# Taking the feed-forward halves' work in the order of the source, with weight splits at fixed places

## The chip, the core and the metric

The kernel runs on one core of a Trainium2 chip. Its time is device time in microseconds (us). Before the change it is 2786.39 us, the median of three runs (2783.53 to 2787.11). One further execution was recorded by the hardware profiler; it took 2785.98 us, and all rows shown here come from it.

## The reference, cut to what matters

A trunk of two layers is applied to 640 tokens (512 of a sample, 128 of a prompt) with width D = 1024. Each layer is half a feed-forward sub-layer, a mixer (attention and the like) and another feed-forward half, so there are four feed-forward halves. Each sub-layer is normalised and modulated by a shift, a scale and a gate that are computed from a condition vector.

```python
def swiglu(h, w_in, w_out):                  # w_in: 1024 x 5632, w_out: 2816 x 1024
    gate, up = jnp.split(h @ w_in, 2, axis=-1)
    return (jax.nn.silu(gate) * up) @ w_out

def adaln_sublayer(x, mod, s, g_pre, g_post, fn, weight):
    h = rmsnorm(x, g_pre) * (1 + scale) + shift
    y, aux = fn(h)
    return x + weight * gate * rmsnorm(y, g_post), aux
```

with `mod = silu(cond) @ mod_w[l] + mod_b[l]`: nine vectors of 1024 for each layer and each of two conditions.

## The kernel before

**Numbers and matmuls.** Values are float32. Every operand of a matmul is split into a high part and a remainder (`hi`, `lo`), and a product is made of three passes, hi x hi, hi x lo and lo x hi. The split of a weight block is a cast on ScalarE (ACT, line 159) and a subtraction on VectorE (DVE, line 160). The matmuls run on TensorE (PE).

**Parts and units.** The hidden width of 2816 is 22 slices of 128, called units here, and `PARTS = (2, 4, 4, 4, 4, 4)` groups them. A part computes its units' `g = silu(gate) * up` and then multiplies them with the rows of w_out that belong to them, in output products over five token tiles and two halves of the columns (matmuls of line 779, sums into `yacc` on DVE at line 804, in part 0 copies on ACT at line 802). Between the groups of output products there are places at which other things are traced: one group of matmuls, then `stream.pump()`, then `tick()`.

**Part 0** uses plain column products (matmuls of line 607) and `glu` (lines 650 to 652), whose result is split into g's two parts. `combine` then makes sums and differences of the activations' quarters (lines 662 and 665, two of the sums on GpSimd (POOL), the others on DVE) and splits them. Its eight steps are taken one at a place by `tick()`, between part 0's output products.

**Parts 1 to 5** compute gate and up of a unit together, in `strassen`, by a scheme of seven products p1, p2, p6, p5, p7, p4, p3 instead of eight, each of twelve matmuls of 128x128 by 128x320 (line 690). The order on PE for unit i of a part is p2 of i, p3 of i-1, p6, p5, p7 of i, p1 of i+1, p4 of i. p1 and p2 use one weight block of the unit (kind X), p6 one called S, p5 and p4 one called Z, p7 and p3 one called V. p1's sum is copied by ACT (line 709), p2's is added by DVE and passed through SiLU (lines 714 and 715), p6 writes onto p1's bank and ACT copies it (line 720) before p7 may write there, p7's sum is copied and added (lines 730 and 731), p4's is multiplied in (line 736), p3's is added, passed through SiLU and multiplied (lines 744 to 746). The two halves of the unit's g are then cast and subtracted (lines 352 and 353 through `out`). Behind the last unit of a part stands `fill`, the first group of output matmuls, between its p7 and p4.

**The stream of weights.** `Stream` keeps a list of all weight blocks in the order of use. Raw blocks of 512 KB are loaded over SyncE's (SP's) DMA queue into three buffers; a new load is issued when a buffer's count says that one is free. For a unit two raw blocks are loaded (gate and up), and four POOL operations (line 145) combine them into S and V's source as soon as X is split, in place in the raw buffers. `split()` makes the high and the low part of the next block in one of five buffers (`W_BUFS`). `pump()` is called between products, and also by `done()` at the end of the products that free a block. Each call splits all blocks for which there is room, but stops behind a block of a unit.

**Modulation.** The vectors for later sub-layers are computed beside the feed-forward halves, by `tick()`. `on_v` works on DVE (lines 411 and 413, 16 products of 128x512) and ends in a short PE matmul (line 425), an addition (line 428) and writes on SP's queue; one such unit is staged behind every part but the last, over the places of the output products. `on_t` works on PE (line 445, two bursts of 16 small matmuls) and is staged over the places of `strassen` in some parts. Both load their weights over SP's queue.

**What sets the order of the work.** The program is traced in the order of the source. Then a scheduler with a model of costs sets the order of each engine's instructions; within what the data allow it may put an instruction that is traced later ahead of one that is traced earlier. Each engine, and each queue that issues DMAs, then takes its instructions in that order, one after the other.

Of the kernel before, what the change touches and what calls it, by code (L numbers as in the profile page):

```python
# [60 lines left out]
class Stream:  # L61
# [9 lines left out]
    def __init__(self, nc, raw_pool, w_pool, late):  # L71
# [6 lines left out]
        self.limit = W_BUFS  # L78
        self.part_tile = None

    def add(self, key, spec):

        self.loads.append(spec)
        self.specs.append((key, spec[:2], "W", (len(self.loads) - 1,)))

    def add_unit(self, key, gate, up):
        n = len(self.loads)
        self.loads += [gate, up]
        for kind in self.UNIT:
            self.specs.append(((kind, *key), (4 if kind == "S" else 8, 128), kind, (n, n + 1)))  # L90
# [16 lines left out]
    def _room(self):  # L107
        if self.n_split == len(self.specs):
            return False
        key, _, kind, lids = self.specs[self.n_split]  # L110
        if key in self.late:
            return key in self.extra
        if len(self.held) >= self.limit:
            return False
        if kind == "S":
            return lids[0] in self.parts and self.n_pump >= self.parts[lids[0]][1] + PARTS_LAG
        return True

    def pump(self):

        self.n_pump += 1
        self._loads()
        while self._room():
            kind = self.specs[self.n_split][2]
            self.split()
            self._loads()
            self._combine()
            if kind in self.UNIT:
                break
        self._combine()  # L130

    def _combine(self):
# [58 lines left out]
def kblock(w, k0, nk, c0, n):  # L191
    return w[k0 * 128:(k0 + nk) * 128, c0:c0 + n].rearrange("(k p) n -> p k n", p=128)
# [22 lines left out]
def hybrid_flow_kernel(ctx: ExitStack, tc: tile.TileContext, I, O):  # L215
    nc = tc.nc
# [21 lines left out]
    stream = Stream(nc, wpool, wpool, late)  # L238
# [16 lines left out]
    def ffn_specs(l, j):  # L255
        wi, wo = I["ffn_w_in"][l, j], I["ffn_w_out"][l, j]
        first = not specs
        if first:

            for q in range(NK // 2):  # L260
                srcs = [(0, 128, 256 * u, kblock(wi, 2 * q, 2, u * D_FF, 256)) for u in range(2)]
                stream.add(("first", q), (2, 512, srcs))
        for p, fts in enumerate(ffn_parts()):
            for f in fts if p or not first else ():
                gate, up = (whole(kblock(wi, 0, 8, u * D_FF + f * 128, 128)) for u in range(2))
                if p:
                    stream.add_unit((l, j, f), gate, up)
                else:
                    stream.add(("in", l, j, f, 0), gate)
                    stream.add(("in", l, j, f, 1), up)  # L270
            if p < len(PARTS) - 1:
                for h in range(2):
                    for f in fts[::2]:
                        stream.add(("out", l, j, f, h), whole(kblock(wo, f, 2, h * 512, 512)))
            else:
                for f in fts:
                    stream.add(("out", l, j, f), whole(kblock(wo, f, 1, 0, 1024)))
# [69 lines left out]
    hT = [state.tile([128, NK, TOK], F32R, name=f"hT{i}") for i in range(2)]  # L347
    modrows = [[dram.tile([2, D], F32, name=f"mod{l}_{r}") for r in range(9)] for l in range(2)]
    nc.scalar.activation(out=cc, in_=craw, func=AF.Silu)

    def split(src, hi, lo):
        a = nc.scalar.copy(hi, src)  # L352
# [267 lines left out]
    def ffn(fp, l, s, pending, todo, nxt, banks0=None):  # L620
# [4 lines left out]
        j = s // 2  # L625
# [53 lines left out]
        class Unit:  # L679


            count = 0

            def __init__(self, f, g, pos, last):
                self.f, self.g, self.pos, self.last = (l, j, f), g, pos, last
# [32 lines left out]
            def p6(self):  # L718
                self.product(self.Y, self.get("S"), C[2], False)
                nc.scalar.copy(self.t[:, 1], self.Y)  # L720
                self.done("S")

            def p5(self):
# [17 lines left out]
            def p3(self):  # L741
                t = self.t
                self.product(self.Z, self.half(self.V, 1), B[1, 1], False)
                nc.vector.tensor_tensor(out=t[:, 1], in0=t[:, 1], in1=self.Z, op=ALU.add)
                nc.scalar.activation(out=t[:, 1], in_=t[:, 1], func=AF.Silu)
                nc.vector.tensor_tensor(out=t[:, 1], in0=t[:, 1], in1=t[:, 2], op=ALU.mult)
                self.out(1 if self.last else 0, 2)
                self.done("V")

            def out(self, a, b):  # L750
# [6 lines left out]
        def strassen(fts, g, fill):  # L757

            us = [Unit(f, g, i, f == fts[-1]) for i, f in enumerate(fts)]
            for i, u in enumerate(us):  # L760
                todo = [] if i else [u.p1]
                todo += [u.p2] + ([us[i - 1].p3] if i else []) + [u.p6, u.p5, u.p7]
                todo += [us[i + 1].p1, u.p4] if i + 1 < len(us) else [fill, u.p4, u.p3]
                for fn in todo:
                    fn()
                    stream.pump()
                    tick()

        stream.part_tile = part_tile
        for p, fts in enumerate(parts):  # L770
            last = p == len(parts) - 1
# [13 lines left out]
            if not last:  # L785
# [22 lines left out]
                fill = lambda: next(outs)  # L808
            else:
# [23 lines left out]
                def reload(ts, tags):  # L833
                    for t, tag in zip(ts, tags):
                        x[t] = fp.tile([128, 4, HALF], F32, tag=tag, name=tag, bufs=1)
                        x[t] = x[t].rearrange("p k n -> p (k n)")[:, 0:D]
                        src = x_saved[t]
                        if first:
                            src = I["x_sample"][0, t * 128:(t + 1) * 128, :] if t < 4 else I["x_prompt"][0]
                        nc.sync.dma_start(out=x[t], in_=src)  # L840
# [5 lines left out]
            if p == 0 and first:  # L846
                for i in range(len(fts)):
                    glu(banks0[i], g, i)
                prep += combine()
            elif p == 0:  # L850
                banks = [pair_banks() for _ in fts]
                win = []
                for i, f in enumerate(fts):
                    for u in range(2):
                        win.append(stream.get(("in", l, j, f, u)))
                        col_product(win[-1], banks[i][u], 0)
                        if (i, u) == (0, 1):
                            pending[0]()
                        elif (i, u) == (1, 0):
                            pending[1]()  # L860
                for i, f in enumerate(fts):
                    for u in range(2):
                        col_product(win[2 * i + u], banks[i][u], 1)
                        if u == 1:
                            glu(banks[i], g, i)
                        stream.done()
                prep += combine()
            else:
                if not last:
                    mod.stage("t", n_t[p], 7 * len(fts))  # L870
                strassen(fts, g, fill)
            if p == 3 and first:
                spread_bias(g[0][0])
            if not last:
                mod.stage("v", 1, 4 * len(fts) - 1)
                for _ in outs:
                    stream.pump()
                    tick()

        reload((4,), ("b40",))  # L880

        def pieces(t):
# [1284 lines left out]
```

## Time and profile before

| | |
|---|---|
| median of 3 runs | 2786.39 us (2783.53 to 2787.11) |
| profiled execution | 2785.98 us |
| its span in the trace | 2784.2 us |
| PE busy | 2563.5 us, 92% |
| DVE busy | 1845.4 us, 66% |
| ACT busy | 1178.1 us, 42% |
| POOL busy | 703.3 us, 25% |
| bytes moved by DMA | 296.95 MB, 107 GB/s on average |

The span runs from the first to the last instruction on the trace. PE is the engine of matmuls; "PEld", its loading of weights, runs beside it. "PEclk" in the profile is the clock that was granted to PE, as a share of full speed. A row of a timeline gives the start and the duration of an instruction, with its line in the kernel; "<-" names what it waited for. A row of the table of windows gives a stretch of the span, its length, the busy time and number of instructions of PE, PEld, DVE, ACT and POOL in it, the granted clock, the busy share of the DMA engines and GB/s. A row of SP's queue is the issue of a transfer (line 99 loads raw weight blocks). Idle time of an engine that nothing waits for costs nothing.

### The profile page before, as it was taken

The numbers are of one execution on the slowest core, as the hardware profiler recorded it, in microseconds if no ns is written. First come the engines' busy times: TensorE is split into PE (matmuls) and PEld (weight loads), VectorE is DVE, ScalarE is ACT, GpSimd is POOL, SyncE is SP. The second block draws the span as 40 slices with busy tenths as digits, with TensorE's granted clock in tenths as the row PEclk, the third lists the DMA queues.
The fourth block names the chain that finished last, engine by engine and source line by source line (L and its number), as shares of the span: only waits on it lengthen the run. The fifth ranks groups of instructions, "written<-read, shape, count | busy, mean of one in ns | idle before, by whom it ended". The sixth has DMA issues, their size and how long they took to land.

```text
span 2784.2 us, 40608 instructions
## 1 busy us (share of the span) xinstructions
PE 2563.5 (92%) x15930; PEld 2275.5 (82%) x15930; DVE 1845.4 (66%) x2847; ACT 1178.1 (42%) x2179; POOL 703.3 (25%) x612
## 2 busy tenths in 40 slices
PE   6898979999999989999988999999899998999998
PEld 5787868888866878888877888888899977888887
DVE  5766555675676676667568665676777768755556
ACT  4433323464455543333354333334655655333333
POOL 1222322310010032223233223123433302323222
PEclk9999999999999999999999999999999999999999
DMA  8345453421210433443343543444122223322233
GB/s 247 116 132 155 143 163 98 137 68 48 65 40 16 132 98 117 138 126 85 99 136 116 163 125 107 117 127 133 57 65 76 66 97 123 93 84 61 77 105 114
DMA packets 356697, 296.95 MB, mean 107 GB/s; under 512 B 44365, under 2 KB 289049, under 8 KB 356505
## 3 DMA queue, kind: packets, MB, share of 16 engines
q1 hardware_dynamic: 352040, 281.25, 34.0%
q10 hardware_dynamic: 2880, 9.18, 0.8%
q0 software_dynamic: 1584, 3.93, 0.5%
q8 instruction: 125, 2.05, 0.3%
q14 instruction: 68, 0.55, 0.1%
HBM read 282.24 MB, written 15.97 MB: 107 GB/s over the span
## 4 chain that ended last, share of the span: by engine, by line
PE 42%; DVE 11%; POOL 6%; ACT 4%; issue 3%; DMA 2%; DVEq 0%; ACTq 0%; POOLq 0%; SPq 0%
PE ps L690 15%; PE ps L779 13%; PE ps L607 5%; DVE wlo L160 3%; PE ps L1023 3%; POOL raw L145 3%; PE ps L597 2%; ACT whi L159 2%; POOL G L145 2%; DVE mod L413 1%; PE ps L1970 1%; DVE mod L411 1%; ACT g L352 1%; DMA mod<-in_mod_w_dram 1%; PE ps L1951 1%
## 5 line engine op out<-in xcount | busy, mean ns | idle before, releaser
L159 ACT CAST whi<-raw 128x1024 fp32r<-128x1024 f32 x400 | 418.7, 1050 | 475.9 <-PE ps L779 225.1
L779 PE MATMUL ps<-whi,g 128*128 128x512 f32 x1760 | 574.6, 403 | 40.3 <-ACT g L352 26.6
L160 DVE TENSOR_TENSOR wlo<-raw,whi 128x1024 fp32r<-128x1024 f32 x400 | 495.8, 1242 | 140.2 <-ACT whi L159 129.9
L690 PE MATMUL ps<-hT,whi 128*128 128x320 f32 x2560 | 577.1, 313 | 0.0
L145 POOL TENSOR_TENSOR raw<-raw 128x512 f32<-128x512 f32 x160 | 216.7, 1354 | 1241.2 <-DVE wlo L160 1138.3
L690 PE MATMUL ps<-b,whi 128*128 128x320 f32 x1920 | 444.4, 319 | 93.0 <-ACT xn L720 51.0
L690 PEld LDWEIGHTS ps<-hT,whi 128*128 128x128 f32 x2560 | 433.1, 191 | 12.9 <-DVE x L804 5.3
L779 PEld LDWEIGHTS ps<-whi,g 128*128 128x128 f32 x1760 | 339.7, 193 | 122.6 <-ACT g L352 29.4
L690 PEld LDWEIGHTS ps<-b,whi 128*128 128x128 f32 x1920 | 329.7, 194 | 110.4 <-ACT xn L720 61.3
L690 PE MATMUL ps<-hT,wlo 128*128 128x320 f32 x1280 | 399.6, 312 | 0.0
L779 PE MATMUL ps<-wlo,g 128*128 128x512 f32 x880 | 353.7, 402 | 0.0
L690 PE MATMUL ps<-b,wlo 128*128 128x320 f32 x960 | 303.6, 316 | 12.1 <-DVE wlo L160 12.1
L607 PE MATMUL ps<-hT,whi 128*128 128x384 f32 (+1 forms) x1216 | 277.9, 317 | 0.0
L690 PEld LDWEIGHTS ps<-hT,wlo 128*128 128x128 f32 x1280 | 244.4, 191 | 0.0
L607 PEld LDWEIGHTS ps<-hT,whi 128*128 128x128 f32 x1216 | 204.2, 189 | 21.9 <-issue 15.2
L413 DVE SCALAR_TENSOR_TENSOR mod<-mod,cc 128x512 f32<-128x512 f32 x238 | 201.0, 880 | 17.7 <-DMA mod<-in_mod_w_dram 17.7
L779 PEld LDWEIGHTS ps<-wlo,g 128*128 128x128 f32 x880 | 170.0, 193 | 37.4
L690 PEld LDWEIGHTS ps<-b,wlo 128*128 128x128 f32 x960 | 186.2, 194 | 12.4 <-DVE wlo L160 12.4
L607 PE MATMUL ps<-hT,wlo 128*128 128x384 f32 (+1 forms) x608 | 188.8, 311 | 0.0
L804 DVE TENSOR_TENSOR x<-x,ps 128x512 f32<-128x512 f32 x160 | 107.6, 685 | 92.2 <-PE ps L779 91.5
L159 ACT CAST whi<-G 128x512 fp32r<-128x512 f32 x72 | 44.7, 621 | 263.5 <-POOL G L145 152.5
L160 DVE TENSOR_TENSOR wlo<-G,whi 128x512 fp32r<-128x512 f32 x72 | 73.0, 1014 | 118.3 <-ACT whi L159 118.1
(407 smaller groups left out, 3911.0 us busy)
## 6 DMA issues: line engine op xcount, KB each, us to landing
raw<-in_ffn_w_in_dram SPq DMA_DIRECT2D x172, 512.0 KB
mod<-in_mod_w_dram SPq DMA_DIRECT2D x128, 512.0 KB
raw<-in_ffn_w_out_dram SPq DMA_DIRECT2D x88, 512.0 KB
raw<-in_na_w_qkv_dram SPq DMA_DIRECT2D x24, 512.0 KB
raw<-in_ab_w_in_dram SPq DMA_DIRECT2D x22, 512.0 KB
raw<-in_mod_w_dram SPq DMA_DIRECT2D x32, 256.0 KB
xs<-x ACTq DMA_DIRECT2D x15, 512.0 KB
b<-xs SPq DMA_DIRECT2D x15, 512.0 KB
```

Of the source, the lines that this page charges most:

```text
L145: self.nc.gpsimd.tensor_tensor(out=out, in0=in0, in1=in1, op=op)
L159: self.nc.scalar.copy(hi[:, :k * n], raw[:, :k * n])
L160: self.nc.vector.tensor_tensor(out=lo[:, :k * n], in0=raw[:, :k * n], in1=hi[:, :k * n].bitcast(F32), op=ALU.subtract)
L352: a = nc.scalar.copy(hi, src)
L411: nc.vector.tensor_scalar(out=acc[:, c], in0=raw[:, 0], scalar1=w, scalar2=None, op0=ALU.mult)
L413: nc.vector.scalar_tensor_tensor(out=acc[:, c], in0=raw[:, k % 2], scalar=w, in1=acc[:, c], op0=ALU.mult, op1=ALU.add)
L597: nc.tensor.matmul(out=banks[grp], lhsT=w[a][:, k, :], rhs=hT[b][:, k, o:o + n], start=(k == 0 and (a, b) == (0, 0)), stop=(k == NK - 1 an ...
L607: nc.tensor.matmul(out=banks[grp], lhsT=w[a][:, k, :], rhs=hT[b][:, k, o:o + n], start=(k == 0 and (a, b) == (0, 0)), stop=(k == NK - 1 an ...
L690: nc.tensor.matmul(out=out, lhsT=w[a][:, k, :], rhs=b[c][:, k, :], start=start and (k, a, c) == (0, 0, 0), stop=(k == 3 and (a, c) == PASS ...
L779: nc.tensor.matmul(out=out, lhsT=g[a][kf][:, t * 128:(t + 1) * 128], rhs=w[b], start=(kf == 0 and (a, b) == (0, 0)), stop=(kf == len(fts) ...
L804: nc.vector.tensor_tensor(out=dst, in0=dst, in1=acc[t], op=ALU.add)
L1023: nc.tensor.matmul(out=y[t][h], lhsT=hT[a][:, k, t * 128:(t + 1) * 128], rhs=ws[k // 2, h][b][:, k % 2, :], start=(k == 0 and (a, b) == (0 ...
```

## The change

A unit's four blocks are no longer split wherever `pump()` finds room. Only a part's first unit (`alone`) may be split so; any of its blocks that are still missing are split behind p1 and p2 of that unit. For the other units the source names the places: behind p2 of a unit two blocks (its own Z and V), behind p6 one (X of the next unit), behind p4 one (S of the next unit). Blocks of w_out are still split by `pump()` and `done()`. The split of the second half of g that p3 ends with is traced behind the copy in the next unit's p6 (`Unit.later`), except in a part's last unit. And `in_order` ties each instruction that is traced after part 0's activation (`mark`) to the one traced before it on the same engine, without a semaphore, up to the end of the last part's output matmuls: within that stretch of each feed-forward half the scheduler can no longer change the order on any engine.

```diff
     def _room(self):
@@
-        if len(self.held) >= self.limit:
+        if len(self.held) >= self.limit or (kind in self.UNIT and lids[0] not in self.alone):
             return False
@@
+    def unit_item(self):
+
+        kind = self.specs[self.n_split][2]
+        assert kind in self.UNIT and len(self.held) < self.limit, (self.specs[self.n_split], self.held)
+        self.split()
+        self._loads()
         self._combine()
@@
-                    stream.add_unit((l, j, f), gate, up)
+                    stream.add_unit((l, j, f), gate, up, f == fts[0])
@@
+    def in_order(last):
+
+        traced = nc.cur_bb.bb.instructions
+        n = next(i for i in reversed(range(len(traced))) if traced[i] is last) + 1
+        before = {}
+        for i in traced[:n]:
+            before[i.engine] = i
+        for i in traced[n:]:
+            if i.engine in before:
+                tc.add_manual_dep(
+                    i, before[i.engine].name,
+                    mybir.DependencyInfo(mybir.DependencyClass.NoSync, mybir.DependencyReason.DATA), reason="in_order",
+                )
+            before[i.engine] = i
@@
             def p6(self):
                 self.product(self.Y, self.get("S"), C[2], False)
                 nc.scalar.copy(self.t[:, 1], self.Y)
+                for fn in Unit.later:
+                    fn()
+                Unit.later.clear()
                 self.done("S")
@@
-                self.out(1 if self.last else 0, 2)
+                if self.last:
+                    self.out(1, 2)
+                else:
+                    Unit.later.append(lambda: self.out(0, 2))
                 self.done("V")
@@
         def strassen(fts, g, fill):
 
             us = [Unit(f, g, i, f == fts[-1]) for i, f in enumerate(fts)]
+            item = stream.unit_item
             for i, u in enumerate(us):
-                todo = [] if i else [u.p1]
-                todo += [u.p2] + ([us[i - 1].p3] if i else []) + [u.p6, u.p5, u.p7]
-                todo += [us[i + 1].p1, u.p4] if i + 1 < len(us) else [fill, u.p4, u.p3]
-                for fn in todo:
+                begin, end = i == 0, i + 1 == len(us)
+
+                todo = [(u.p1, ())] if begin else []
+                todo.append((u.p2, () if begin else (item, item)))
+                if not begin:
+                    todo.append((us[i - 1].p3, ()))
+                todo += [(u.p6, () if end else (item,)), (u.p5, ()), (u.p7, ())]
+                todo.append((fill if end else us[i + 1].p1, ()))
+                todo.append((u.p4, () if end else (item,)))
+                if end:
+                    todo.append((u.p3, ()))
+                for fn, items in todo:
                     fn()
+                    while begin and fn in (u.p1, u.p2) and stream.specs[stream.n_split][0][1:] == u.f:
+                        item()
+                    for split_next in items:
+                        split_next()
                     stream.pump()
                     tick()
@@
                 strassen(fts, g, fill)
+            if p == 0:
+                mark = nc.cur_bb.bb.instructions[-1]
@@
+        in_order(mark)
         reload((4,), ("b40",))
```

## Rows read from the trace of the kernel before

**Rows 1.** page, busy time by engine: us, share of the span, instructions

```profile
PE 2563.5 (92%) x15930; PEld 2275.5 (82%) x15930; DVE 1845.4 (66%) x2847; ACT 1178.1 (42%) x2179; POOL 703.3 (25%) x612
```

**Rows 2.** windows: parts 1 to 5 of each half; part 0 of the second

```profile
99.70:542.60 442.90, 394.33 (x2653) 357.32 (x2652) 268.66 (x345) 145.73 (x219) 120.21 (x102) 0.96 0.46 135
1012.30:1421.50 409.20, 382.21 (x2395) 351.86 (x2392) 269.50 (x335) 147.75 (x221) 107.94 (x76) 0.97 0.39 115
1519.80:1932.50 412.70, 385.87 (x2523) 353.74 (x2520) 268.26 (x340) 147.91 (x221) 106.81 (x76) 0.98 0.42 125
2363.90:2750.30 386.40, 367.26 (x2179) 341.13 (x2176) 231.23 (x279) 147.08 (x221) 107.51 (x76) 0.99 0.30 88
988.00:1012.30 24.30, 16.83 (x70) 12.72 (x68) 21.40 (x16) 12.24 (x18) 12.44 (x6) 0.86 0.23 68
```

**Rows 3.** PE's waits: waiting <- ended by: us in total, times, longest

```profile
PE ps L690 <- ACT xn L720: 51.0, 28, 2.9
PE ps L690 <- ACT tok L720: 38.7, 18, 2.6
PE ps L779 <- ACT g L352: 26.6, 7, 7.5
...
PE ps L690 <- DVE wlo L160: 12.1, 1, 12.1
```

**Rows 4.** timeline of PE, one unit of the fourth half: start, duration, instruction

```profile
2461.51 0.45 PE L690 MATMUL ps<-b,whi 128*128 128x320 f32 x2
...
2463.26 0.46 PE L690 MATMUL ps<-hT,whi 128*128 128x320 f32 x2
...
2470.15 0.31 PE L690 MATMUL ps<-hT,wlo 128*128 128x320 f32 x1
2471.96 0.57 PE L690 MATMUL ps<-b,whi 128*128 128x320 f32 x2 [1.50 <-ACT tok L720]
```

**Rows 5.** timeline of ACT, a part's end and the same unit

```profile
2415.99 1.05 ACT L159 CAST whi<-raw 128x1024 fp32r<-128x1024 f32 x1 [0.41 <-DMA raw<-in_ffn_w_out_dram]
...
2470.34 0.62 ACT L159 CAST whi<-G 128x512 fp32r<-128x512 f32 x1 [2.00 <-POOL G L145]
2470.86 0.72 ACT L352 CAST g<-xn 128x640 fp32r<-128x640 f32 x1
2471.49 0.42 ACT L720 COPY tok<-ps 128x320 f32<-128x320 f32 x1
```

**Rows 6.** timeline of DVE, the same stretch

```profile
2402.80 1.91 DVE L353 TENSOR_TENSOR g<-tok,g 128x640 fp32r<-128x640 f32 x1
...
2412.63 1.23 DVE L160 TENSOR_TENSOR wlo<-raw,whi 128x1024 fp32r<-128x1024 f32 x1
2413.77 0.48 DVE L744 TENSOR_TENSOR xn<-xn,ps 128x320 f32<-128x320 f32 x1
...
2418.21 0.82 DVE L353 TENSOR_TENSOR g<-xn,g 128x640 fp32r<-128x640 f32 x1
...
2463.46 0.49 DVE L736 TENSOR_TENSOR xn<-xn,ps 128x320 f32<-128x320 f32 x1 [2.57 <-PE ps L690]
```

**Rows 7.** timeline of SP's DMA queue, the load of that part's end

```profile
2412.15 0.37 SPq L99 DMA_DIRECT2D raw<-in_ffn_w_out_dram  x1
```

**Rows 8.** timeline of PE, modulation matmuls in the first half

```profile
228.19 1.08 PE L445 MATMUL ps<-mod,cc 128*32 128x128 f32 x32
```

**Rows 9.** timeline of DVE, fourth half, ahead of part 0

```profile
2318.16 0.88 DVE L411 TENSOR_SCALAR mod<-mod,cc 128x512 f32<-128x512 f32 x2 [3.11 <-DMA mod<-in_mod_w_dram]
...
2328.36 1.48 DVE L662 TENSOR_TENSOR xn<-hT,hT 128x1280 f32<-128x1280 f32 x1
...
2334.08 2.07 DVE L413 SCALAR_TENSOR_TENSOR mod<-mod,cc 128x512 f32<-128x512 f32 x3
```

**Rows 10.** timeline of POOL, fourth half, part 0 and part 1

```profile
2344.56 3.32 POOL L662 TENSOR_TENSOR tok<-hT,hT 128x1280 f32<-128x1280 f32 x1
...
2402.29 1.74 POOL L145 TENSOR_TENSOR raw<-raw,G 128x512 f32<-128x512 f32 x1
```

More of the change, by code (lines that the diff above doesn't have):

```diff
@@ L79, in __init__ @@
         self.part_tile = None
+        self.alone = set()
     def add(self, key, spec):
@@ L84, in add, with add_unit @@
         self.specs.append((key, spec[:2], "W", (len(self.loads) - 1,)))
-    def add_unit(self, key, gate, up):
+    def add_unit(self, key, gate, up, alone):
         n = len(self.loads)
+        if alone:
+            self.alone.add(n)
         self.loads += [gate, up]
@@ L129, in pump @@
                 break
+        self._combine()
+    def unit_item(self):
[3 more added lines that the diff above has]
+        self._loads()
         self._combine()
@@ L679, in ffn @@
         class Unit:
-            count = 0
+            count, later = 0, []
             def __init__(self, f, g, pos, last):
```

## The prediction

> **What bounds the kernel now.** I read the page's busy line first: TensorE (PE) is busy for 92% of the span, VectorE (DVE) for 66%, ScalarE (ACT) for 42% [rows 1]. So only gaps of PE are worth time, and what fills one must not open another. The table of stretches cuts out what the change orders: in each feed-forward half parts 1 to 5 (Strassen products and the output products behind them) and, ahead of them, the first part's output products, "part 0" [rows 2]. PE is idle there (length less PE busy) for 48.6, 27.0, 26.8 and 19.1 us in the parts of the four halves, 121.5 us together, and for 7.5 us in part 0 of the second half. Elsewhere nothing is changed. The list of PE's waits says on whom: 46 waits, 89.7 us, on ACT's copy of line 720, that is of p6 ahead of p7; 26.6 us on ACT's cast of g; once 12.1 us on a weight split [rows 3].
>
> In the timelines one such wait can be followed: p5's last matmul starts at 2470.15 and p7's first at 2471.96 instead of 2470.30, so 1.66 us are lost where the row says 1.50 [rows 4]. On ACT the copy stood behind the split of the *next* unit's S, which had itself waited 2.00 us for GpSimd (POOL), and behind a 640-column cast of g [rows 5]. That is a wrong order in a queue, not a lack of an engine, and source order puts the copy first.
>
> **The change, part by part.** All durations are from one execution, 2785.98 us (span 2784.2), 0.41 us under the median of 2786.39; the sum is made on 2786.
>
> *Removed.* In the parts 121.5 us of idle time, with 0.16 more for each of about 50 waits (1.66 against 1.50): 129.5 us. The single wait of 12.1 us is among them: there a run of modulation products stood ahead of the split on DVE, which source order excludes.
>
> *Added: a unit walked in source order.* Time 0 is the end of p2 of unit i. A product takes 1.75 (2461.51 to 2463.26 [rows 4]), 1.76 with its restart; a consumer starts 0.20 after the product's slot (2463.46 [rows 6]). An ACT operation lets the next start 0.09 before its end (2470.86 and 0.72, then 2471.49 [rows 5]); a 1024-column cast takes 1.05, its subtraction 1.23, of which it holds DVE for 1.14 [rows 5, 6]. In the source stand p2 with its add and SiLU, then split Z, split V, then p3 of unit i-1 with its add and SiLU, then p6 with its copy.
> - Add from 0.20 to 0.69, SiLU from 0.74; cast Z 1.11 to 2.16, cast V from 2.06. DVE subtracts Z from 2.21, V from 3.35, and only at 4.49 comes to p3's add, whose product ended at 1.76. SiLU 5.02, and behind it the copy of p6: 5.39 to 5.81. p7 is due at 3 x 1.76 = 5.28 and starts at 5.86: **0.58 lost**.
> - The chain goes on: multiply to 6.02, cast of g from 6.07 (0.62), then cast X of unit i+1 from 6.69 to 7.74, subtraction to 9.02. Product p1 of unit i+1 is due at 7.62; its third matmul reads wlo at 9.07 instead of 7.91: **1.16 lost**. So an inner unit loses 1.74 where it loses 1.66 now: the old wait goes and two smaller ones come.
> - The last unit of a part: behind its Z and V come the out-projection blocks, which every done() still splits. The first was loaded long before. The second is loaded only when Z's subtraction has freed a raw buffer, at 3.44, and its cast stands right behind p3, ahead of the copy of p6. Such a load landed 3.84 after its issue (2412.15; the cast waited for it until 2415.99 [rows 5, 7]). Cast from 7.31, copy 8.26 to 8.68, p7 at 8.73 instead of 5.28: **3.45 lost**. Today Z is split a unit earlier, and the block is there in time. Bounds: 0 (it has landed) and 7.3 (another block goes first, 3.84 more).
>
> A part of four units without modulation matmuls loses 2 x 1.74 + 3.45 = 6.93 (its first unit's blocks are split in the stretch before). There are 9 of these: 62.4. Where one modulation unit is computed on PE, in bursts of 1.08 together [rows 8], the bursts hide about half of the inner losses: 5.4, in 7 parts 37.8. Four parts (three in the first half, one in the third) have two such units: there SP, in order, issues a modulation block only behind the unit's two raw blocks, and PE waits for it in order. Three blocks land between 3.84 (side by side) and 11.5 (one after the other); with 7.7 I take 5 of them as seen by PE (bounds 0 and 8): 4 x 10.4 = 41.6. In 13 output stretches a matmul at the end waits in order for DVE's modulation products; I take 1 each (0, since no such wait stands among the long ones of these stretches today, to 3): 13. Together 154.8, so the parts come out at **+25**.
>
> *Part 0.* Here DVE sets the pace: busy for 21.4 of 24.3 us in the second half [rows 2]. Today it does 12 of its 16 modulation products and both first sums of the Strassen combinations *before* part 0, while PE works on the column products: from 2318.16 to 2336.07, 2 x 0.4, 10 x 0.67 and 2 x 1.41, 10.3 us [rows 9]. In source order all of them stand behind the mark. Up to the modulation matmul that PE must pass, DVE then has: the rest of g 1.1, 7 combination steps x 1.41, 16 products at 0.67, S, Z and V 2.9, so 24.6; with some 5 of waiting for POOL's two sums of 3.32 [rows 10] and 1.5 for ACT it is 31, against 24.3 now. PE's wait for g goes (the splits that stood ahead of glu's SiLU come behind it), but the one for the modulation is longer. +7 in three halves, +3.5 in the first, where only four products were done ahead: **+24.5**. DVE's free time before it gives perhaps 3 back to the column products. Bounds of part 0: -22 (only the waits for g count) and +45 (POOL's sums fully in the way).
>
> That DVE and POOL stop each other shows in the rows: a 640-column subtraction takes 0.82 us alone and 1.91 us with POOL's operation of 1.74 beside it [rows 6, 10]. The Trainium skill ("SBUF — State Buffer", "SBUF: two separate sides") says that their shared port is locked for a whole instruction and not divided. The rows agree. By that rule alone POOL's sums would be paid in full, 6.6 us and not 5, and the total would be 6 us higher; it speaks against packing DVE's work behind them.
>
> *Clock.* The mean granted clock is 0.96, 0.97, 0.98 and 0.99 in the parts [rows 2], lowest where PE idled most: for some of the time it was at 1.2 GHz and not at 2.4. A loss of 4, 3, 2 and 1% is 42 us at most. 46 waits of 1.95 us on average go, 24 of 3.5 to 6 and some 30 near 0.6 come. I take 0, bounds -15 and +25.
>
> *Error of the walk.* Walked in the order that the rows show today, a unit loses 1.9 where they show 1.66; so I take 0.2 off each of about 60 walked waits: -12.
>
> Sum: 25 + 24.5 - 3 - 12 = +34.5, on 2786: **2820 us**.
>
> **Rivals.**
> - *The blocks land in time*: 20 x 3.45 = 69 goes, 2751. For it: a load could find a free buffer earlier. Against: of three raw buffers one is filled and two are freed by the very splits that now stand later.
> - *The change does what the waits promise*: the 89.7 and 12.1 us go and nothing comes, 2684. For it: PE is the only full engine. Against: the walk's two waits need no accident.
> - *Nothing moves*: part 0 costs nothing, since PE no longer waits for g (24.5 - 3), and the waits for modulation products don't show (13): 2820 - 34.5 = 2785.5. For it: DVE has 34% free. Against: not in these stretches.
> - *SP's queue decides*: in order, one load or small write that waits holds every raw block behind it. From 3 us more per part in the 15 parts of the first three halves: 2865.
> - That the change doesn't do what it says: an engine's order is fixed in the program; I give it nothing.
>
> **How the numbers follow.** A measurement of this kernel can tell about 0.2%, 5.6 us, from no change. Forecast 0.48 (its own range 2796 to 2848: landing of the last unit's block, part 0), SP's queue 0.17, blocks in time 0.15, nothing moves 0.12, promise kept 0.08. Faster takes the blocks in time, the promise and 0.01 of "nothing moves": 0.24; within 0.2%: 0.09; slower 0.67. The range leaves out the promise kept and the tail of SP's queue: 2745 to 2872.
>
> **What would show it.** In the profile after: about 20 waits of PE of 3 to 4 us on the copy in p6, each behind a cast of an out-projection block that waits for its DMA, and about 30 near 0.6; short waits on wlo in p1; in part 0 one long wait at line 425's matmul with DVE busy throughout; the wait of 12.1 us and the casts of S ahead of the copy gone. The prediction is wrong if p7 of a part's last unit starts on time, or if part 0 is no longer than 25 us.

## The result and the profile after

The changed kernel takes 2890.15 us (median of 4 runs, 2887.15 to 2898.53) against 2786.75 for the kernel before in the same runs: a ratio of 1.0375, 95% interval 1.035 to 1.0401, slower by 103 us. The forecast of 2820 and the range up to 2872 are both too low. The profiled execution has a span of 2888.2 us, 104.0 more than before.

The page's busy line of the kernel after (us, share of the span, instructions) is to be read against [rows 1]:

```profile
PE 2595.2 (90%) x15930; PEld 2295.2 (79%) x15930; DVE 1796.6 (62%) x2847; ACT 1163.5 (40%) x2179; POOL 666.4 (23%) x612
```

The same 15930 matmuls keep PE busy 31.7 us longer, and its idle time (span less busy) rises from 220.7 to 293.0 us, by 72.3. Both have to be found. The windows of the kernel after, cut at the same places as [rows 2] (parts 1 to 5 of the four halves, then part 0 of the second; columns as there):

```profile
105.70:562.00 456.30, 406.01 (x2649) 368.82 (x2648) 255.81 (x343) 143.47 (x220) 114.68 (x103) 0.93 0.45 132
1039.20:1459.75 420.55, 387.45 (x2393) 353.66 (x2392) 257.93 (x336) 143.68 (x220) 99.26 (x76) 0.96 0.38 112
1561.60:1994.20 432.60, 393.87 (x2521) 358.87 (x2520) 258.41 (x340) 143.50 (x220) 99.11 (x76) 0.95 0.41 121
2434.00:2854.30 420.30, 384.04 (x2177) 351.69 (x2176) 222.42 (x280) 143.58 (x220) 97.27 (x76) 0.96 0.27 82
1006.80:1039.20 32.40, 15.96 (x70) 11.48 (x68) 30.94 (x29) 12.47 (x18) 10.04 (x4) 0.77 0.29 81
```

Length less PE busy: PE idles in the parts for 50.3, 33.1, 38.7 and 36.3 us, 158.4 together, against 121.5. The parts are 78.6 us longer: 36.9 of idle time and 41.7 of busy time at a lower granted clock. Part 0 of the second half, from its first output product to p1, takes 32.4 us instead of 24.4, with DVE busy for 30.9 of them; over the four halves part 0 is 31.3 us longer (7.4, 8.0, 8.0, 7.9). The rest of the program gives 5.9 back. 78.6 + 31.3 - 5.9 = 104.0.

PE's waits in the kernel after (line 747 is p6's copy, 452 the matmul that ends a modulation unit on DVE, 472 the modulation matmuls on PE, 172 the subtraction of a split) are to be read against [rows 3]:

```profile
PE ps L717 <- ACT tok L747: 76.6, 29, 4.2
PE ps L452 <- DVE mod L440: 63.0, 4, 16.1
PE ps L717 <- ACT xn L747: 33.9, 13, 8.8
PE ps L472 <- DMA mod<-in_mod_w_dram: 27.5, 10, 7.0
...
PE ps L717 <- DVE wlo L172: 20.3, 36, 0.7
...
PE ps L825 <- ACT g L379: 1.1, 1, 1.1
```

The wait on the cast of g (26.6 us) and the single one of 12.1 us are gone, as the order promised. The copy of p6 is waited for longer than before, 110.5 us instead of 89.7. The 63.0 us of line 452 (6.4 before) and the 27.5 us of line 472 (0.9 before) are nearly all new, and so are 36 short waits on the subtraction.

**The last part's start.** This is the place that the prediction does not have. The window of the first half's last part (p1 to the first output products), before and then after:

```profile
487.90:542.60 54.70, 51.63 (x347) 50.55 (x344) 34.45 (x42) 25.05 (x39) 16.85 (x12) 1.00 0.43 118
```

```profile
492.10:562.00 69.90, 56.95 (x347) 54.55 (x344) 33.56 (x46) 24.45 (x39) 15.20 (x12) 0.90 0.43 108
```

The same 347 matmuls, 15.2 us more, 5.3 of them PE's busy time. DVE there, in the kernel after (start, duration):

```profile
500.84 2.52 DVE L520 SCALAR_TENSOR_TENSOR G<-G,tok 128x1024 f32<-128x1024 f32 x2 [7.53 <-DMA G<-mod]
504.17 0.17 DVE L507 SCALAR_TENSOR_TENSOR mcol<-mcol,gcol 128x8 f32<-128x8 f32 x1 [0.81 <-DMA mcol<-mod]
505.42 0.17 DVE L507 SCALAR_TENSOR_TENSOR mcol<-mcol,gcol 128x8 f32<-128x8 f32 x1 [1.08 <-DMA mcol<-mod]
505.50 0.48 DVE L741 TENSOR_TENSOR xn<-xn,ps 128x320 f32<-128x320 f32 x1
```

Lines 520 and 507 belong to `load_gate` and `load_pre`, which stand in the source ahead of the last part's products. Their vectors are still on the way. In the kernel before, DVE took p2's sum (line 714) ahead of the gate that is still being loaded (line 493):

```profile
491.84 0.49 DVE L714 TENSOR_TENSOR xn<-xn,ps 128x320 f32<-128x320 f32 x1 [2.00 <-PE ps L690]
...
499.29 1.23 DVE L493 SCALAR_TENSOR_TENSOR G<-G,tok 128x1024 f32<-128x1024 f32 x1 [2.51 <-DMA G<-mod]
```

In order, p2's sum (line 741) may not pass them, though its product ended long before; behind it stand the SiLU and the copy of p6 on ACT, and p7 on PE:

```profile
506.02 0.47 ACT L742 ACTIVATE xn<-xn 128x320 f32<-128x320 f32 x1 [11.37 <-DVE xn L741]
506.39 0.41 ACT L747 COPY xn<-ps 128x320 f32<-128x320 f32 x1
```

```profile
499.15 0.31 PE L717 MATMUL ps<-hT,wlo 128*128 128x320 f32 x1
506.85 0.90 PE L717 MATMUL ps<-b,whi 128*128 128x320 f32 x2 [7.40 <-ACT xn L747]
507.55 0.47 PE L717 MATMUL ps<-b,wlo 128*128 128x320 f32 x1
```

The four halves lose 7.40, 6.58, 8.79 and 5.62 us so, 28.4 together. And behind the wait a single matmul takes 0.47 us instead of 0.31. The granted clock (third number from the end) was 1.00, that is 2.4 GHz, ahead of the wait and is 0.50, that is 1.2 GHz, behind it:

```profile
490.00:498.00 8.00, 8.00 (x56) 7.01 (x55) 3.31 (x5) 0.48 (x2) 0.00 (x0) 1.00 0.55 162
506.80:510.00 3.20, 3.15 (x12) 3.15 (x13) 1.47 (x3) 0.95 (x2) 0.92 (x1) 0.50 0.43 3
```

**The last unit of a part** is as forecast. ACT and then PE in the fourth half, part 1:

```profile
2486.48 1.04 ACT L171 CAST whi<-raw 128x1024 fp32r<-128x1024 f32 x1 [1.22 <-DMA raw<-in_ffn_w_out_dram]
2487.43 0.42 ACT L747 COPY tok<-ps 128x320 f32<-128x320 f32 x1
```

```profile
2487.90 0.56 PE L717 MATMUL ps<-b,whi 128*128 128x320 f32 x2 [4.02 <-ACT tok L747]
...
2489.42 0.47 PE L717 MATMUL ps<-b,wlo 128*128 128x320 f32 x1
```

The cast waits for the out-projection block's load, the copy stands behind it, p7 starts 4.0 us late, and 1.5 us later the matmuls are at 0.47 too. These waits are 3.1 to 4.2 us long.

**Part 0**, second half: PE, DVE and POOL:

```profile
1021.17 0.40 PE L825 MATMUL ps<-whi,g 128*128 128x512 f32 x1
1037.65 1.64 PE L452 MATMUL ps<-mod,ones 128*32 128x256 f32 x8 [16.08 <-DVE mod L440]
```

```profile
1009.79 4.24 DVE L689 TENSOR_TENSOR xn<-hT,hT 128x1280 f32<-128x1280 f32 x1
1013.95 3.57 DVE L438 TENSOR_SCALAR mod<-mod,cc 128x512 f32<-128x512 f32 x2
```

```profile
1009.15 7.70 POOL L689 TENSOR_TENSOR tok<-hT,hT 128x1280 f32<-128x1280 f32 x2
```

The output products end sooner than before, and then PE stands for 16.1 us before the modulation matmul that it must not pass. The two DVE rows beside POOL's two sums take 7.8 us, where such operations take 1.48 and, for the two of the second row, 0.88 alone [rows 9].

### The profile page after: what moved, and what is told of

The parts are those of the page before. It is cut to its first block, busy times and chain, and to the rows that moved or that the text cites. A ratio compares the mean times of both kernels' runs of the same rounds, so it can differ in the third digit from the quotient of the medians.

```text
span 2888.2 us, 40550 instructions
## 1 busy us (share of the span) xinstructions
PE 2595.2 (90%) x15930; PEld 2295.2 (79%) x15930; DVE 1796.6 (62%) x2847; ACT 1163.5 (40%) x2179; POOL 666.4 (23%) x612
## 4 chain that ended last, share of the span: by engine, by line
PE 41%; DVE 14%; ACT 5%; DMA 4%; issue 3%; POOL 1%; SPq 1%; ACTq 0%; DVEq 0%; POOLq 0%
PE ps L717 14%; PE ps L825 12%; DVE wlo L172 6%; PE ps L634 4%; PE ps L624 4%; ACT whi L171 4%; PE ps L1072 3%; DMA raw<-in_ffn_w_out_dram 2%; DVE mod L440 1%; PE ps L2019 1%; PE ps L2000 1%; DVE xn L689 1%; PE ps L569 1%; POOL tok L548 1%; DMA mod<-in_mod_w_dram 1%
## 5 line engine op out<-in xcount | busy, mean ns | idle before, releaser
L172 DVE TENSOR_TENSOR wlo<-raw,whi 128x1024 fp32r<-128x1024 f32 x400 | 482.8, 1225 | 245.6 <-ACT whi L171 237.5
L717 PE MATMUL ps<-b,whi 128*128 128x320 f32 x1920 | 461.1, 328 | 110.5 <-ACT tok L747 76.6
L157 POOL TENSOR_TENSOR raw<-raw 128x512 f32<-128x512 f32 x160 | 208.8, 1305 | 1410.7 <-DVE wlo L172 1157.0
L171 ACT CAST whi<-raw 128x1024 fp32r<-128x1024 f32 x400 | 409.5, 1045 | 268.8 <-PE ps L825 198.6
L717 PEld LDWEIGHTS ps<-hT,whi 128*128 128x128 f32 x2560 | 432.9, 191 | 16.0 <-issue 10.8
L717 PEld LDWEIGHTS ps<-b,whi 128*128 128x128 f32 x1920 | 344.6, 202 | 125.8 <-ACT tok L747 84.2
L717 PE MATMUL ps<-hT,wlo 128*128 128x320 f32 x1280 | 405.1, 317 | 20.3 <-DVE wlo L172 20.3
L634 PE MATMUL ps<-hT,whi 128*128 128x384 f32 (+1 forms) x1216 | 277.9, 316 | 0.0
L717 PEld LDWEIGHTS ps<-hT,wlo 128*128 128x128 f32 x1280 | 243.6, 190 | 32.0 <-DVE wlo L172 29.7
L634 PEld LDWEIGHTS ps<-hT,whi 128*128 128x128 f32 x1216 | 204.1, 189 | 21.9 <-issue 15.2
L717 PEld LDWEIGHTS ps<-b,wlo 128*128 128x128 f32 x960 | 194.1, 202 | 0.0
L440 DVE SCALAR_TENSOR_TENSOR mod<-mod,cc 128x512 f32<-128x512 f32 x238 | 183.6, 824 | 1.2 <-DMA mod<-in_mod_w_dram 1.2
L624 PE MATMUL ps<-hT,whi 128*128 128x384 f32 (+1 forms) x640 | 140.7, 311 | 1.6 <-DVE hT L380 1.6
L634 PEld LDWEIGHTS ps<-hT,wlo 128*128 128x128 f32 x608 | 114.6, 188 | 1.1 <-issue 0.8
L624 PEld LDWEIGHTS ps<-hT,whi 128*128 128x128 f32 x640 | 107.5, 190 | 2.9 <-DVE hT L380 2.5
```

Of the source, the lines that this page charges most:

```text
L157: self.nc.gpsimd.tensor_tensor(out=out, in0=in0, in1=in1, op=op)
L171: self.nc.scalar.copy(hi[:, :k * n], raw[:, :k * n])
L172: self.nc.vector.tensor_tensor(out=lo[:, :k * n], in0=raw[:, :k * n], in1=hi[:, :k * n].bitcast(F32), op=ALU.subtract)
L440: nc.vector.scalar_tensor_tensor(out=acc[:, c], in0=raw[:, k % 2], scalar=w, in1=acc[:, c], op0=ALU.mult, op1=ALU.add)
L624: nc.tensor.matmul(out=banks[grp], lhsT=w[a][:, k, :], rhs=hT[b][:, k, o:o + n], start=(k == 0 and (a, b) == (0, 0)), stop=(k == NK - 1 an ...
L634: nc.tensor.matmul(out=banks[grp], lhsT=w[a][:, k, :], rhs=hT[b][:, k, o:o + n], start=(k == 0 and (a, b) == (0, 0)), stop=(k == NK - 1 an ...
```

## The experiments

All of them are edits of the kernel after, or of a kernel named. Idle is the span less PE's busy time; both are of the one profiled execution, which lies up to 8 us off the median (e9_pefree: 2756.39).

| kernel | median us | ratio to before (95%) | PE idle | PE busy |
|---|---|---|---|---|
| before | 2785.76 to 2788.22 | | 220.7 | 2563.5 |
| after | 2890.15 | 1.0375 (1.035 to 1.0401) | 293.0 | 2595.2 |
| e1_free | 2740.73 | 0.984 (0.9824 to 0.9856) | 190.9 | 2546.6 |
| e2_mark | 2857.99 | 1.0257 (1.0238 to 1.0276) | 257.7 | 2599.8 |
| e3_gates | 2851.26 | 1.0239 (1.022 to 1.0258) | 265.5 | 2580.4 |
| e4_hold | 2820.56 | 1.0129 (1.0108 to 1.015) | 249.4 | 2565.6 |
| e5_all | 2757.70 | 0.9895 (0.9875 to 0.9914) | 190.4 | 2563.4 |
| e6_dvefree | 2841.40 | 1.0189 (1.017 to 1.0207) | 239.0 | 2600.3 |
| e7_acttied | 2726.60 | 0.9778 (0.9755 to 0.98) | 164.6 | 2559.8 |
| e8_acthold | 2733.93 | 0.9803 (0.9784 to 0.9822) | 171.6 | 2564.3 |
| e9_pefree | 2748.41 | 0.9862 (0.9844 to 0.988) | 183.9 | 2570.7 |
| e10_dose4 | 2819.26 | 1.0111 (1.0096 to 1.0126) | 225.4 | 2589.9 |
| e11_dose8 | 2855.59 | 1.0244 (1.0227 to 1.0261) | 263.5 | 2590.2 |
| e12_dose12 | 2897.54 | 1.0396 (1.0379 to 1.0413) | 301.0 | 2594.4 |

**e1_free: the places without the order.**

```diff
-        in_order(mark)
```

> The changed kernel without the ties of in_order: the splits stay at the fixed places, but the scheduler may order every engine again. Theory (the order costs, by waits of DVE and PE behind instructions that the scheduler used to move): part 0 comes back to 24 to 25 us from 32, the last part to 55 to 58 from 66 to 72, and the time to 2786 +- 15. Rival (the fixed places cost): it stays at 2860 or more, with the waits on p6's copy still there.

2740.73 us, which is 30 under the lower end of what was expected: part 0 is back at 23.5 to 24.1 us, the last part at 53.4 to 54.0. The change's two halves have opposite signs: the fixed places (with the later split of g) gain some 45 us, the order costs some 150. The waits on the cast of g (26.6 us) and the one of 12.1 us are back as well, so it was the order that had removed them. PE's waits on p6's copy, in this kernel:

```profile
PE ps L717 <- ACT xn L747: 30.2, 26, 2.3
PE ps L717 <- ACT tok L747: 30.1, 29, 2.6
```

60.3 us against 89.7 before, and 16.9 us less busy time.

**e2_mark: part 0 not tied.**

```diff
             else:
                 strassen(fts, g, fill)
-            if p == 0:
-                mark = nc.cur_bb.bb.instructions[-1]
@@
                 for _ in outs:
                     stream.pump()
                     tick()
+            if p == 0:
+                mark = nc.cur_bb.bb.instructions[-1]
```

> The changed kernel with the mark put behind part 0's output products, so that only parts 1 to 5 are tied. Theory (PE's in-order modulation matmul waits for DVE's products and combinations, 63 us in 4 waits): part 0 falls from 31 to 32.4 us to 24 to 25.5 in each half, 2860 (2850 to 2868). Rival (the DVE work only moves on into part 1): part 1 becomes longer by what part 0 gains, 2880 or more.

2857.99 us, 32 less, and part 0 takes 23.9 to 25.5 us; the waits on line 452 are 7.3 us in all. Part 1 did not become longer (88.5 us in the second half, 88.7 with the mark early), so the work was not pushed on into it. The theory holds.

**e3_gates: the last part's gates later on DVE, their loads where they were.**

```diff
     def load_gate(l, s, weight, later=None):
@@
-            nc.vector.scalar_tensor_tensor(out=g, in0=g, scalar=weight, in1=gp, ...)
+            on_dve = lambda g=g: nc.vector.scalar_tensor_tensor(out=g, in0=g, scalar=weight, in1=gp, ...)
+            on_dve() if later is None else later.append(on_dve)
@@ (load_pre likewise)
-                G = load_gate(l, s, 0.5)
+                G = load_gate(l, s, 0.5, gates)
@@ def p7(self):
+                for fn in gates[:1 if self.pos == 0 else None]:
+                    gates.remove(fn)
+                    fn()
```

> The changed kernel with the DVE operations of load_gate and load_pre in the last part traced behind p7 of its first and second unit; their loads stay where they are on SP's queue. Theory (DVE, in order, waits at the start of the last part for vectors that are still being loaded, and p2's sum, its SiLU and p6's copy wait behind it): the waits of 5.6 to 8.8 us on p6's copy go, -28 us, and PE's busy time in the four last parts falls from 226 to 210 or less since the clock is no longer down behind them: 2850 (2840 to 2864). Rival (SP's queue holds it: the raw blocks stand behind the small loads): PE waits as long a product or two later, 2880 or more.

2851.26 us, 39 less: 27.5 of idle time and 14.8 of busy time in the profile. The first half's last part (p1 to the first output products) in this kernel:

```profile
484.20:545.80 61.60, 54.59 (x347) 52.04 (x344) 35.56 (x46) 24.58 (x39) 18.04 (x12) 0.97 0.49 123
```

8.3 us shorter than in the kernel after, the granted clock 0.97 instead of 0.90. SP's queue was not touched, so it was DVE's order and not SP's. Of PE's busy time only 8 us came back in the four last parts themselves (226 to 218), less than the 16 expected; the last unit's wait still stands there, and without it too (e5) they are at 214.

**e4_hold: one out-projection block less ahead of the copy.**

```diff
                 for fn, items in todo:
+                    stream.limit = W_BUFS - 1 if end and fn.__name__ in ("p2", "p3", "p6") and fn != u.p3 else W_BUFS
                     fn()
@@ def p6(self):
                 nc.scalar.copy(self.t[:, 1], self.Y)
+                stream.limit = W_BUFS
```

> The changed kernel with one buffer less for the stream from p2 to p6's copy of a part's last unit, so that only one out-projection block is split ahead of that copy. Theory (the second block's cast waits for its load ahead of the copy): the 20 waits of 3.1 to 4.1 us at the last unit's p7 fall to 0.6 or less, about -55, and the clock gives up to 10 more: 2830 (2818 to 2845). Rival (the block is then late where it is used): a wait of 2 us or more at the output products, 2870 or more.

2820.56 us, 70 less, the largest single gain. The last units' waits fall from 3.1 to 4.2 us to 1.5 to 1.8, and not to 0.6, so the idle time falls by 43.6 and not by 55:

```profile
PE ps L717 <- ACT tok L747: 35.5, 29, 1.8
```

The busy time falls by 29.6, three times what was allowed for the clock. No wait appeared at the output products of line 825: nothing needed the block so early.

**e5_all: the three together.**

> The changed kernel with the three edits of e2, e3 and e4 together: mark behind part 0's output products, the last part's gate operations behind p7, one buffer less up to the last unit's p6 copy. Theory (three separate places): the gains of 32, 39 and 70 us add up, 2890 - 141 = 2749 (2738 to 2762). Rival (one wait hides another, or the clock's part is counted twice): 2770 or more.

2757.70 us, 132 less than the kernel after, within the range for independent places and 9 above the sum. Source order on all engines in parts 1 to 5 is faster than before (ratio 0.9895), once these three are out of the way, but still 17 us slower than the same places without the order (e1).

**e6, e7, e9: which engine's ties cost.** Each is the kernel after with one line of `in_order` changed, here that of e7:

```diff
-            if i.engine in before:
+            if i.engine in before and i.engine == mybir.EngineType.Activation:
```

> The changed kernel with all engines tied but DVE. Theory (the losses in part 0 and at the last part's start come from DVE's ties, those at the last unit from ACT's cast behind a load): part 0 is 24 to 26 us again, the last part's first wait goes, the 20 waits of 3 to 4 us at the last unit stay: 2890 - 32 - 39 = 2819 (2805 to 2835). Rival (PE's own order holds part 0, and SP's the last part): part 0 stays at 30 or more, 2850 or more.

2841.40 us, above the range. Part 0 is 26.9 and the last part about 60 us, so those two losses are DVE's, as expected; but the waits on the copy at the last units are still there (64.1 us in 20), and PE waits for splits for 44.0 us, where it did for 20.3 with DVE tied: a free DVE takes part of the gain back.

> The changed kernel with ACT alone tied. Theory (ACT's order sets both the gain at the inner units, since the copy of p6 no longer stands behind the cast of S, and the loss at the last unit, where it stands behind the second out-projection block): against the untied kernel at 2741, the 55 waits on the copy of 60 us become 20 of about 3 us and 40 of about 0.6, 84 us: 2765 (2750 to 2785). Rival (with DVE and SP free the block's load is issued a unit earlier and lands in time): the waits of 3 us don't appear, 2735 or less.

2726.60 us, the fastest of all, 2.2% under before: the rival's number, but not by its mechanism. The block is as late as ever. ACT in the fourth half, part 1:

```profile
2368.74 1.05 ACT L171 CAST whi<-raw 128x1024 fp32r<-128x1024 f32 x1 [2.89 <-DMA raw<-in_ffn_w_out_dram]
2369.70 0.41 ACT L747 COPY tok<-ps 128x320 f32<-128x320 f32 x1
```

PE at the same time:

```profile
2366.47 0.86 PE L825 MATMUL ps<-whi,g 128*128 128x512 f32 x3
...
2369.59 0.40 PE L825 MATMUL ps<-wlo,g 128*128 128x512 f32 x1
2370.16 0.56 PE L717 MATMUL ps<-b,whi 128*128 128x320 f32 x2 [0.17 <-ACT tok L747]
```

The scheduler, which knows ACT's order, put 14 output matmuls of line 825, traced behind p7, into the wait. p7 starts 0.17 us late.

> The changed kernel with all engines tied but PE. Theory (the late copy of p6, the late modulation products and the late DVE work at the last part's start stay, but PE may put other ready matmuls into the wait): the 20 waits at the last unit are filled by the first output matmuls, -65 with the clock, and part 0's matmul of the modulation moves behind part 1's first products, some -15; the last part's start stays: 2890 - 80 = 2810 (2790 to 2830). Rival (the other engines' ties hold PE's other work as well): 2850 or more.

2748.41 us, 62 under the forecast. PE's waits:

```profile
PE ps L452 <- DVE mod L440: 64.6, 6, 16.3
PE ps L717 <- ACT xn L747: 33.2, 13, 8.5
...
PE ps L717 <- ACT tok L747: 10.3, 25, 1.5
...
PE ps L472 <- DMA mod<-in_mod_w_dram: 2.6, 5, 1.0
```

The waits at the last unit are filled (10.3 us left), and also those on modulation loads (2.6 instead of 27.5), which I had left out. Part 0 is unmoved at 32.4 us: the scheduler kept the modulation matmul ahead of part 1. So freeing PE alone undoes the whole loss and more, though ACT and DVE are as late as before in part 0 and at the last part's start.

**e8_acthold: e7 with the edits of e2 and e4.**

> ACT alone tied, the mark behind part 0's output products, and one buffer less up to the last unit's p6 copy. Theory (ACT's order pays once the second out-projection block stands behind the copy): waits on the copy under 35 us, 2715 (2700 to 2730), under the untied kernel's 2741. Rival (the scheduler gives the time back on DVE or PE): 2735 or more.

2733.93 us, above the range and 1 us under the rival's bound, and not faster than e7. No wait on the copy is left at all, but with PE free they were 7.4 us in all in e7 already: the later split had next to nothing to give.

**e10 to e12: longer waits on purpose.** In e5_all, the copy of p6 in a part's last unit is written four, eight or twelve times more:

```diff
-                nc.scalar.copy(self.t[:, 1], self.Y)
+                for _ in range(5 if self.last else 1):
+                    nc.scalar.copy(self.t[:, 1], self.Y)
```

> The kernel of e5_all with the copy of p6 written four times more in the last unit of each part (same values), some 1.3 us later. Theory of the clock (matmuls behind a wait run at 1.2 GHz once the wait is long enough): PE's idle time rises by 26 us and its busy time by 10 to 20; 2795. Rival (the clock doesn't hang on these waits): idle +26, busy +-3, 2784.

> The kernel of e5_all with the copy of p6 written eight times more in the last unit of each part, some 2.6 us later. Theory of the clock: idle +52, busy +30, as much as the changed kernel lost at waits of 3 to 4 us: 2840. Rival: idle +52, busy +-3, 2810.

> The kernel of e5_all with the copy of p6 written twelve times more in the last unit of each part, some 3.9 us later. Theory of the clock: idle +78, busy no more than with eight (+30), since the half-clock stretch behind a wait doesn't grow with the wait: 2866. Second theory (the clock's price grows with the wait): busy +45, 2880. Rival: busy +-3, 2836.

The 20 waits are 1.5 to 1.8 us in e5_all, then 3.3 to 3.6, 5.2 to 5.4 and 7.0 to 7.2. The busy lines of the four kernels, in that order:

```profile
PE 2563.4 (93%) x15930; PEld 2261.0 (82%) x15930; DVE 1805.7 (66%) x2847; ACT 1160.4 (42%) x2179; POOL 682.0 (25%) x612
```

```profile
PE 2589.9 (92%) x15930; PEld 2288.8 (81%) x15930; DVE 1807.3 (64%) x2847; ACT 1195.2 (42%) x2259; POOL 682.2 (24%) x612
```

```profile
PE 2590.2 (91%) x15930; PEld 2289.4 (80%) x15930; DVE 1808.6 (63%) x2847; ACT 1229.0 (43%) x2339; POOL 682.5 (24%) x612
```

```profile
PE 2594.4 (90%) x15930; PEld 2293.6 (79%) x15930; DVE 1807.7 (62%) x2847; ACT 1262.1 (44%) x2419; POOL 682.1 (24%) x612
```

The idle time rises by 35, 73 and 111 us, more than expected since a copy holds ACT longer than I had taken. All three times are above the forecasts. The busy time rises by 26.5 with the first step (10 to 20 expected) and then hardly: 26.8 and 31.0 in all. That is 1.3 us for each of the 20 waits, paid in full at 3.4 us and hardly again for longer ones. The theory of the clock holds, in its first form. By the granted clock of the trace, the matmuls in the 8 us behind the wait run at 1.2 GHz, for a while, after 5 of the 20 waits in e5_all (each of the 5 was 1.75 us long), after 19 in e10_dose4 and after all 20 in the other two. So a wait of 1.6 us is mostly, not always, without this price. The rows show it directly, PE in e5_all and then in e10_dose4 at a last unit's p7:

```profile
2546.68 0.56 PE L719 MATMUL ps<-b,whi 128*128 128x320 f32 x2 [1.56 <-ACT tok L749]
2547.07 0.31 PE L719 MATMUL ps<-b,wlo 128*128 128x320 f32 x1
```

```profile
2599.89 0.90 PE L719 MATMUL ps<-b,whi 128*128 128x320 f32 x2 [3.39 <-ACT tok L750]
2600.60 0.47 PE L719 MATMUL ps<-b,wlo 128*128 128x320 f32 x1
```

## Why the prediction was wrong

It said 2786 + 34.5, of which +13 in the parts (25 less 12 for the walk's error), +24.5 in part 0, -3 elsewhere and 0 for the clock. Measured are +78.6, +31.3 and -5.9. The parts' 78.6 are 8.5 of idle time for what was walked, 28.4 for the last part's start, and 41.7 of busy time. By the trace's granted clock, matmuls in the parts run at 1.2 GHz for 64.2 us before and for 135.7 after; there one of 320 columns follows the next by 0.267 us, at 2.4 GHz by 0.147. So some 32 of the 41.7 (an estimate: 71.5 us at that ratio) are the clock's, and the other 10 stay open.

- *The step that failed first: the term "Clock", "I take 0, bounds -15 and +25".* The mean clock of [rows 2] was priced per stretch, and the waits that go and come were netted against each other. But they differ in kind: those that went were 1.95 us on average, those that came are 3 us and more. Of the 42 waits on the copy that are longer than 1 us in the kernel before, 13 have matmuls at 1.2 GHz behind them; of the 24 in the kernel after, 23. And 20 waits of 3.4 us cost 1.3 us of busy time each more than 20 of 1.6 us (e10). Measured: 41.7 us of busy time in the parts, 31.7 in all, since elsewhere the clock is down for less time than before.
- *The step that was missing:* "Source order" was walked for units, splits and modulation, but not for `load_gate` and `load_pre`, which the scheduler used to move back on DVE. 28.4 us of idle time, and more by the clock; taken away by e3.
- *The last unit:* 3.45 forecast, 3.1 to 4.2 measured, by the mechanism named; shown by e4. The rival that the blocks land in time is refuted.
- *The inner units:* 0.58 and 1.16 forecast, 0.4 to 0.6 and at most 0.70 measured. They were forecast at 53 us in all, 45 with the 0.2 taken off each, and take 29.0 (8.7 on the copy, 20.3 on the subtraction): too much by 16, which hid part of what was missing elsewhere.
- *Modulation units on PE:* 5 us for each of four parts forecast, 27.5 in all measured on line 472. *At the output stretches*, 13 forecast, none measured.
- *Part 0:* "31, against 24.3" came out at 32.4 (30.9 in the first half), DVE busy throughout. The 3.5 for the first half was too little: it lost 7.4 as well. DVE's waiting for POOL's two sums was put at 5: the two rows beside them take 7.8 us instead of 2.4, 5.4 more.
- *The rival "SP's queue decides"* (2865) comes nearest by its number, but not by its mechanism: in e5 SP's queue is still tied in parts 1 to 5, and the time is 2757.70. What its order can have cost at line 472 is the 27.5 us.
- *That a wait is a loss at all* was assumed as soon as the order was fixed. With PE's ties alone removed (e9) the same late copies at the last units cost almost nothing (those at the last part's start still cost their wait). PE's ties turn lateness into loss; ties on ACT alone (e7) are a gain.

By the rule of the Trainium skill ("SBUF — State Buffer", "SBUF: two separate sides"), which has the port that DVE and POOL share locked for a whole instruction, the prediction would have paid POOL's two sums in full, 6.6 us and not 5. The rows of part 0 show 5.4. They agree with the lock all the same: POOL's first sum ends at 1012.67, DVE's sum 1.36 us later, POOL's second sum 2.82 us after that (the shortest such sum of any run takes 2.88), DVE's next operation 0.28 us later again. The two engines take turns, and DVE loses what is left of POOL's operation when its own comes up, not all of it.

Of the matmul time at 1.2 GHz in the kernel after, 82.9 us stand in the 8 us behind the 20 waits at the last units and 17.7 behind the four at the last part's start, so the last units have most of the clock's price. What stays open is how the two share it in time: e4 gives 29.6 us of busy time back and e3 14.8, together more than e5_all with both (31.8).

## What to carry to other kernels

Before an order is fixed, list every instruction that the scheduler moved against the source, on each engine, not only those of the loop that is looked at: here the consumers of small loads, ahead of a loop, cost 28.4 us of waiting. Fix the order of the engine whose order is wrong (here ACT's) and leave the engine that must stay busy free to fill waits. And count waits by length: here one of 1.6 us mostly cost itself alone, and one of 3.4 us cost 1.3 us more.

## What was unexpected of the hardware

Behind a wait of 3.4 us PE's matmuls of 128x320 took 0.47 us instead of 0.31 for some microseconds, and the extra cost did not grow with the wait: 26.5 us for 20 waits of 3.4 us, 31.0 for 20 of 7.1. The same holds for the 16.1 us of waiting in part 0. The first 9 us of part 1 in the second half, in the kernel after and then in e2_mark, where that wait is gone:

```profile
1039.20:1048.20 9.00, 9.00 (x56) 8.98 (x55) 5.01 (x6) 3.53 (x5) 0.00 (x0) 0.87 0.18 47
```

```profile
1024.40:1033.40 9.00, 9.00 (x65) 9.00 (x62) 3.75 (x5) 3.64 (x6) 0.73 (x1) 1.00 0.00 1
```

PE gets through 56 matmuls instead of 65, at a granted clock of 0.87 instead of 1.00. Nine matmuls at 0.147 us are 1.3 us: no more behind 16.1 us than behind 3.4. PE's busy time over the whole program does not show this gain (it is 4.6 us higher in e2), so the stretch itself has to be looked at.
